# Routed experts on one Trainium2 core: the order of the 64-column and 32-column products over four weight blocks, and the places of the three small experts

## The chip, the cores and the metric

The kernel runs on one core of one Trainium2 chip, as a single program. The metric is the device time of one execution in microseconds (us), and less is better. The core's engines are TensorE (PE, with its weight loads shown as PEld), VectorE (DVE), ScalarE (ACT), GpSimd (POOL) and SyncE (SP), which issues nearly all transfers from HBM.

## The reference

A two-layer encoder trunk over 256 tokens of width 1024 in float32. Layer 0 is attention (two kinds of heads) and a dense SwiGLU; layer 1 is dilated window attention and a routed SwiGLU: each token goes to the two of eight experts with the highest router logits. Cut to the part that the change touches:

```python
def one_block(args):                       # the tokens of one expert
    tok, g, e = args
    xb = xt[tok]                           # (tokens, 1024)
    yb = (jax.nn.silu(xb @ wg[e]) * (xb @ wu[e])) @ wd[e]   # 1024 -> 3584 -> 1024
    return (yb.astype(jnp.float32) * g[:, None]).astype(h.dtype)
```

Each expert has 3 x 1024 x 3584 float32 weights, 44 MB, and 64 tokens on the mean. The output is x plus the gated sum of both experts of each token.

## The kernel before

The first third of the time goes to layer 0 and to the attention of layer 1. From 518 us on the kernel works through the eight experts one after another, in **places** e = 0 to 7. Place 0 always holds expert 7 (`FIRST`); the other seven experts are ranked on the chip by the number of their tokens, and `RANK` (line 28) says which rank stands in which place. The three smallest (ranks 0 to 2) stand in the places of `TWO` (line 26). What a place can hold is fixed when the program is built: 64 rows in a place of `TWO`, 96 in the others (`ROOM`, line 29). The shapes of all instructions so depend on the place and not on the data; tokens beyond the room go to `overflow`, behind an `If` at the end.

**Weights.** An expert's weights come as 42 loads of 1 MB each, all in the order of use and all issued on SP (line 221). Sixteen slots of 1 MB hold them (rings of 8, 2, 4 and 2); a load waits until the products that read its slot are done. Each load is two **blocks** of 128 x 1024 columns (`granules`, line 1040): 56 blocks for the gate and up projections (seven groups g of eight) and 28 for the down projection.

**Products.** The tokens are the stationary operand, the weights stream. For each block `products` (line 1278) goes through `parts(e)` (line 1229). The **wide part** takes tokens 0 to 63: two products with 64 stationary columns each, side by side in the array, each with half of the block's columns. A place with room for 96 also has the **narrow part**, tokens 64 to 95: four products with 32 stationary columns side by side, each with a quarter of the columns. float32 products run as two passes each, so in the trace a block is four wide matmuls of 512 columns, and then eight narrow ones of 256. Wide results gather in PSUM tiles psA (gate, up) and psD (down), narrow ones in psB.

**Between them on TensorE.** After each group g ScalarE and VectorE make h (lines 1310, 1311), and `turn` (line 1286) transposes it, with three 128-column products in a place with a narrow part and two in the others (line 1292). As written, `turn(g-1)` stands behind the fourth block of the next group, and `turn(6)` behind the third block of the down projection. `route` (line 1234) gathers the tokens of the next two places with 32 products (line 1251) and some small ones (line 1265); it is called by `ahead` in places 1, 3 and 5, as written behind block 18 of the down projection. At the end of a place `scatter` (line 1322) scales the result and adds it to the output by one indirect transfer for each part.

**Order.** Each engine runs its queue in order. The queue is laid out when the program is built, by a planner that goes through the instructions as they are written, but puts a later one ahead of an earlier one if, by the planner's own estimate of times, the earlier one still waits for its data. So the order in the trace can differ from the written one.

Of the kernel before, what the change touches and what calls it, by code (L numbers as in the profile page):

```python
# [20 lines left out]
KD = 8  # L21
# [1 line left out]
NE = 8  # L23
EPS = 1e-6
BIG = 4096.0
TWO = (1, 3, 5)
FIRST = NE - 1
RANK = (-1, 0, 3, 1, 4, 2, 5, 6)
ROOM = tuple(64 if j in TWO else 96 for j in range(NE))
RING = 8  # L30
NCONV = 3
# [148 lines left out]
def tile_trunk(ctx, tc, xT_d, fm_d, rw_d, ct_d, ada_et, ada_e, win_ab, win_c, uq_d, ukv_d, wout_e,  # L180
               ffn_gu, ffn_d, ada_ot, ada_o, qkv_d, wout_o, router_d, gu_d, wd_d, out, dbg=None):
    nc = tc.nc
    V, S, G, TE = nc.vector, nc.scalar, nc.gpsimd, nc.tensor
# [9 lines left out]
    def bank(tag):  # L193
        return psum.tile([P, 512], F32, tag=tag, name="ps" + tag, bufs={"A": 2, "D": 1, "B": 3, "C": 2}[tag])
# [40 lines left out]
    def F(n):  # L235
        return fm[:, FM[n][0]:FM[n][1]]
# [28 lines left out]
    for a in range(2):  # L265
        ps = bank("C")
        for b in range(4):
            k = 4 * a + b
# [102 lines left out]
    last = [None]  # L371
# [387 lines left out]
    for a in range(3):  # L759
        g = F("qn")[:, a:a + 1] if a < 2 else F("kvn")  # L760
# [14 lines left out]
    for k in range(2):  # L775
        w = stream.get()
# [14 lines left out]
    w = stream.get()  # L791
    for tt in range(2):
        for a in range(2):
            ps = bank("B")
# [6 lines left out]
    at = ExitStack()  # L801
# [88 lines left out]
    for f in range(22):  # L890
        ps = bank("A").rearrange("p (a b) -> p a b", a=2)
        for m in range(2):
            w = stream.get()
# [87 lines left out]
    at = ExitStack()  # L981
# [58 lines left out]
    def granules(j):  # L1040

        for make in [gu_load(j, g, kq) for g in range(7) for kq in range(4)] + [wd_load(j, pc) for pc in range(14)]:
            w = make()
            for lo in (0, 1024):
                yield w[:, lo:lo + 1024]

    stream.prime()
    first, stream = stream, Stream(cvm, wo[NCONV:])
# [16 lines left out]
    def wout():  # L1065
        for _ in range(NCONV):
            yield first.get()
        cvs.close()
        slots[0] = order()
        while True:  # L1070
            yield stream.get()

    wg = wout()
# [44 lines left out]
    rk8 = mb.tile([P, NE], F32, name="rk8")  # L1118
    for j, r in enumerate(RANK):
        G.memset(rt8[:, j:j + 1], float(r))  # L1120
# [3 lines left out]
    ps = bank("C")  # L1124
# [73 lines left out]
    def gates():  # L1198
# [14 lines left out]
        V.tensor_copy(eid, key)  # L1213
        V.tensor_scalar(cap, rk8, float(len(TWO)) - 0.5, -32.0, op0=ALU.is_lt, op1=ALU.mult)
        V.tensor_scalar(cap[:, :NR], cap[:, :NR], 96.0, None, op0=ALU.add)
# [13 lines left out]
    def parts(e):  # L1229


        return ((0, 64, 2),) if e in TWO else ((0, 64, 2), (64, 32, 4))

# [38 lines left out]
    def expert(e, xg, lo, mid, ahead):  # L1272


        wg = granules(e)
        hh, hts = {}, {}

        def products(outs, x, w, m, start, stop):
            for ps, (at, n, q) in zip(outs, parts(e)):
                c = 1024 // m // q  # L1280
                wv = w.rearrange("p (m c) -> p m c", m=m)
                for j in range(q):
                    TE.matmul(ps[n * j:n * j + n, :m * c].rearrange("p (m c) -> p m c", m=m), x(at, n),  # L1283
                              wv[:, :, j * c:(j + 1) * c], start=start, stop=stop, tile_position=(0, n * j))

        def turn(g):

            h = hh.pop(g)
            pt = bank("C")
            nb = 2 if e in TWO else 3  # L1290
            for b in range(nb):
                TE.transpose(pt[:, b * P:(b + 1) * P], h[:, b * P:(b + 1) * P], ident)  # L1292
            ht = mt.tile([P, 4, 96], F32, tag="ht%d" % g, name="ht")
            S.copy(ht[:, :, 0:64].rearrange("p (j b) t -> p b j t", b=2),  # L1294
                   pt[:, 0:256].rearrange("p (b j t) -> p b j t", b=2, j=2))
            if nb == 3:
                V.tensor_copy(ht[:, :, 64:96], pt[:, 256:384].rearrange("p (j t) -> p j t", j=4))  # L1297
            hts[g] = ht

        for g in range(7):  # L1300
            ps = [bank("A"), bank("B")][:len(parts(e))]
            for k in range(KD):
                products(ps, lambda at, n: xg[:, k, lo + at:lo + at + n], next(wg), 2, k == 0, k == KD - 1)
                if g and k == 3:
                    turn(g - 1)
                if g == 0 and k == 3 and mid:
                    mid()
            h = mt.tile([P, 384], F32, tag="hh", name="hh", bufs=2)
            for p, (at, w) in zip(ps, ((0, 256), (256, 128))):
                S.activation(h[:, at:at + w], p[:, 0:w], AF.Silu)  # L1310
                V.tensor_tensor(h[:, at:at + w], h[:, at:at + w], p[:, w:2 * w], op=ALU.mult)  # L1311
            hh[g] = h
        Y = [bank("D"), bank("B")][:len(parts(e))]
        for c in range(28):
            if c == 18 and ahead:
                ahead()
            products(Y, lambda at, n: hts[c // 4][:, c % 4, at:at + n], next(wg), 1, c == 0, c == 27)
            if c == 2:
                turn(6)
        return Y  # L1320

# [12 lines left out]
    for e in range(NE):  # L1334
        if e % 2 == 0:
            xg, at, back = nxt.pop()
        ahead = (lambda: nxt.append(route(e + 1))) if e % 2 and e + 1 < NE else None
        scatter(e, expert(e, xg, at[e % 2], None if e else g5_sum, ahead), back[e % 2])
# [104 lines left out]
```

## Time and profile before

| | us |
|---|---|
| runs, median of 3 | 1484.67 (1484.15 to 1487.27) |
| the profiled execution, its own time | 1487.64 |
| its span (first to last instruction) | 1485.8 |
| TensorE busy in the span | 1418.4 (95%) |
| experts, from the first product to the last | 518.4 to 1473.6 |
| weight transfers of the experts | 336 of 1 MB |

The profiled execution is 0.2% above the median. 1.84 us of its time lie outside the span. Matmuls are pipelined, so "busy" says only that some matmul was in flight; how long a block takes is read from where its first matmul and the next block's first matmul start.

### The profile page before, as it was taken

What the parts mean: (1) busy time and instruction counts of PE and PEld (TensorE: products, weight loads), DVE (VectorE), ACT (ScalarE), POOL (GpSimd) and SP (SyncE); (2) the same over time, 40 slices, a digit from 0 to 9 for tenths busy, and PEclk for the clock granted to TensorE, in tenths of its full rate; (3) what the DMA queues carried; (4) which work ended last, traced back from release to release, by engine and by line L of the source; (5) the groups of instructions that cost most, each with busy time, mean ns of one, the idle gap of its engine ahead of it and who ended that gap; (6) DMA issues with size and microseconds to landing.
All of it is one profiled execution on the core that took longest, in us unless ns stands there. A gap on an engine that the chain in (4) does not pass through costs nothing.

```text
span 1485.8 us, 23384 instructions
## 1 busy us (share of the span) xinstructions
PE 1418.4 (95%) x9779; PEld 647.5 (44%) x9779; DVE 433.6 (29%) x964; ACT 354.2 (24%) x750; POOL 51.1 (3%) x51
## 2 busy tenths in 40 slices
PE   6889999999989899999999998999998999999996
PEld 4646999998766722223322222322222322222221
DVE  5866787786886410000000000000000000000000
ACT  4557644445568310000100001100000100000000
POOL 0320000000020000000000000000000000000000
PEclk9989999999999899999999999999999999999998
DMA  9846678788432788999999999999999999999830
GB/s 393 341 155 251 212 285 299 284 306 308 161 114 91 295 336 321 320 331 415 421 418 420 378 331 419 421 417 421 351 333 410 421 414 421 367 326 335 317 140 11
DMA packets 67363, 472.11 MB, mean 318 GB/s; under 512 B 8145, under 2 KB 8593, under 8 KB 11185
## 3 DMA queue, kind: packets, MB, share of 16 engines
q1 hardware_dynamic: 64944, 467.34, 81.5%
q0 software_dynamic: 1872, 2.10, 0.9%
q8 instruction: 79, 1.29, 0.3%
q10 hardware_dynamic: 432, 1.08, 0.2%
q14 instruction: 36, 0.29, 0.1%
HBM read 467.34 MB, written 3.80 MB: 317 GB/s over the span
## 4 chain that ended last, share of the span: by engine, by line
issue 51%; PE 34%; DMA 7%; DVE 5%; ACT 2%; POOL 0%; POOLq 0%; SPq 0%; ACTq 0%; DVEq 0%
DMA out_dram<-acc,row 7%; PE psA L331 6%; PE psA L332 6%; PE psA L333 6%; PE psA L1283 4%; PE psB L1283 3%; PE psD L1283 2%; DVE wlo L355 1%; PE psD L610 1%; PE psB L315 1%; PE psC L596 1%; PE psB L562 1%; PE psA L562 1%; DMA w<-in_ada_ot_dram 1%; PE psC L1251 0%
## 5 line engine op out<-in xcount | busy, mean ns | idle before, releaser
L1283 PE MATMUL psA<-w,xg 128*64 128x512 f32 x1792 | 453.3, 612 | 0.0
L1283 PE MATMUL psD<-w,ht 128*64 128x512 f32 x896 | 229.3, 611 | 0.0
L1283 PEld LDWEIGHTS psA<-w,xg 128*64 128x64 f32 x1792 | 102.3, 136 | 196.9 <-issue 180.1
L1283 PE MATMUL psB<-w,xg 128*32 128x256 f32 x2240 | 180.8, 393 | 0.0
L1310 ACT ACTIVATE hh<-psA 128x256 f32<-128x256 f32 x56 | 21.5, 384 | 603.3 <-PE psA L1283 603.3
L355 DVE TENSOR_TENSOR wlo<-w,whi 128x1024 fp32r<-128x1024 f32 (+2 forms) x119 | 143.8, 1214 | 44.1 <-ACT whi L353 44.1
L1311 DVE TENSOR_TENSOR hh<-hh,psA 128x256 f32<-128x256 f32 x56 | 23.6, 421 | 452.2 <-ACT hh L1310 452.2
L1283 PEld LDWEIGHTS psB<-w,xg 128*32 128x32 f32 x2240 | 44.4, 108 | 227.7 <-issue 227.7
L353 ACT CAST whi<-w 128x1024 fp32r<-128x1024 f32 (+2 forms) x119 | 122.2, 1038 | 74.1 <-issue 30.0
L331 PE MATMUL psA<-h,whi 128*128 128x256 f32 x352 | 97.1, 277 | 0.2 <-ACT h L455 0.2
L332 PE MATMUL psA<-h,whi 128*128 128x256 f32 x352 | 97.1, 277 | 0.0
L333 PE MATMUL psA<-h,wlo 128*128 128x256 f32 x352 | 96.8, 276 | 0.0
L1283 PE MATMUL psB<-w,ht 128*32 128x256 f32 x1120 | 89.5, 391 | 0.0
L1283 PEld LDWEIGHTS psD<-w,ht 128*64 128x64 f32 x896 | 49.6, 135 | 90.2 <-issue 86.9
L1283 PEld LDWEIGHTS psB<-w,ht 128*32 128x32 f32 x1120 | 22.0, 108 | 113.6 <-issue 109.5
L1327 DVE SCALAR_TENSOR_TENSOR acc<-psD,gsl,g5a 128x512 f32<-128x512 f32 x8 | 6.0, 751 | 224.3 <-PE psD L1283 224.3
L331 PEld LDWEIGHTS psA<-h,whi 128*128 128x128 f32 x352 | 66.0, 188 | 0.6 <-ACT h L455 0.4
L332 PEld LDWEIGHTS psA<-h,whi 128*128 128x128 f32 x352 | 65.9, 188 | 0.3 <-DVE h L456 0.2
L333 PEld LDWEIGHTS psA<-h,wlo 128*128 128x128 f32 x352 | 65.9, 188 | 0.0
L1294 ACT COPY ht<-psC 128x256 f32<-128x256 f32 x56 | 20.9, 372 | 169.7 <-PE psC L1292 169.7
L1328 POOL DMA_INDIRECT out_dram<-acc,row x13 | 20.2, 1557 | 959.0 <-DVE acc L1327 923.4
L1297 DVE COPY ht<-psC 128x128 f32<-128x128 f32 x35 | 10.2, 292 | 141.6 <-ACT ht L1294 141.6
(335 smaller groups left out, 1583.5 us busy)
## 6 DMA issues: line engine op xcount, KB each, us to landing
w<-in_gu_dram SPq DMA_DIRECT2D x224, 1024.0 KB, 10.8
w<-in_wd_dram SPq DMA_DIRECT2D x112, 1024.0 KB, 11.1
w<-in_ada_e_dram SPq DMA_DIRECT2D x22, 1024.0 KB, 8.9
w<-in_ffn_gu_dram SPq DMA_DIRECT2D x22, 1024.0 KB, 5.1
w<-in_ada_ot_dram SPq DMA_DIRECT2D x16, 1024.0 KB, 4.9
w<-in_qkv_dram SPq DMA_DIRECT2D x12, 1024.0 KB, 6.6
w<-in_ffn_d_dram SPq DMA_DIRECT2D x11, 1024.0 KB, 6.6
w<-in_ada_o_dram SPq DMA_DIRECT2D x8, 1024.0 KB, 6.3
```

What stands on the lines that cost most here:

```text
L315: behind(TE.matmul(ps[32 * j:32 * j + 32], sc[:, 4 * i + j], w[:, j], start=i == 0, stop=i == 1, tile_position=(0, 32 * j)), after)
L331: TE.matmul(out_, a[0], b[0], start=start, stop=False)
L332: TE.matmul(out_, a[0], b[1], start=False, stop=False)
L333: TE.matmul(out_, a[1], b[0], start=False, stop=stop)
L353: behind(S.copy(hi[:, :n], w), self.after[0])
L355: self.last = V.tensor_tensor(lw, w, hi[:, :n].bitcast(F32), op=ALU.subtract)
L562: TE.matmul(bk[i][:, tt], q[:, tt * P:(tt + 1) * P], k, start=True, stop=True)
L1283: TE.matmul(ps[n * j:n * j + n, :m * c].rearrange("p (m c) -> p m c", m=m), x(at, n), wv[:, :, j * c:(j + 1) * c], start=start, stop=stop, ...
L1294: S.copy(ht[:, :, 0:64].rearrange("p (j b) t -> p b j t", b=2), pt[:, 0:256].rearrange("p (b j t) -> p b j t", b=2, j=2))
L1310: S.activation(h[:, at:at + w], p[:, 0:w], AF.Silu)
L1311: V.tensor_tensor(h[:, at:at + w], h[:, at:at + w], p[:, w:2 * w], op=ALU.mult)
L1328: G.indirect_dma_start(out=out.rearrange("t (j c) -> (t j) c", j=q), out_offset=bass.IndirectOffsetOnAxis(ap=row[:, 0:1], axis=0), in_=ys, ...
```

## The change

Within a group of four blocks all wide products come first, block after block, and then all narrow ones; in the places of `TWO`, which have no narrow part, the products keep their order. `turn(g-1)` is written behind the first four blocks as before, `turn(6)` behind the fourth block of the down projection instead of the third, and `ahead` behind block 16 instead of 18. The places without narrow part become 1, 4 and 7 (they were 1, 3 and 5), and `RANK` is set to fit, so that they still hold the three smallest of the seven ranked experts.

```diff
-TWO = (1, 3, 5)
+TWO = (1, 4, 7)
 FIRST = NE - 1
-RANK = (-1, 0, 3, 1, 4, 2, 5, 6)
+RANK = (-1, 0, 3, 4, 1, 5, 6, 2)
...
-        def products(outs, x, w, m, start, stop):
+        def products(outs, x, ws, m, first, last):
+
             for ps, (at, n, q) in zip(outs, parts(e)):
                 c = 1024 // m // q
-                wv = w.rearrange("p (m c) -> p m c", m=m)
-                for j in range(q):
-                    TE.matmul(ps[n * j:n * j + n, :m * c].rearrange("p (m c) -> p m c", m=m), x(at, n),
-                              wv[:, :, j * c:(j + 1) * c], start=start, stop=stop, tile_position=(0, n * j))
+                for i, w in ws:
+                    wv = w.rearrange("p (m c) -> p m c", m=m)
+                    for j in range(q):
+                        TE.matmul(ps[n * j:n * j + n, :m * c].rearrange("p (m c) -> p m c", m=m), x(i, at, n),
+                                  wv[:, :, j * c:(j + 1) * c], start=i == first, stop=i == last,
+                                  tile_position=(0, n * j))
...
-            for k in range(KD):
-                products(ps, lambda at, n: xg[:, k, lo + at:lo + at + n], next(wg), 2, k == 0, k == KD - 1)
-                if g and k == 3:
+            for k in range(0, KD, 4):
+                products(ps, lambda i, at, n: xg[:, i, lo + at:lo + at + n], [(i, next(wg)) for i in range(k, k + 4)],
+                         2, 0, KD - 1)
+                if g and k == 0:
                     turn(g - 1)
-                if g == 0 and k == 3 and mid:
+                if g == 0 and k == 0 and mid:
                     mid()
...
-        for c in range(28):
-            if c == 18 and ahead:
+        for g in range(7):
+            if g == 4 and ahead:
                 ahead()
-            products(Y, lambda at, n: hts[c // 4][:, c % 4, at:at + n], next(wg), 1, c == 0, c == 27)
-            if c == 2:
+            products(Y, lambda i, at, n: hts[i // 4][:, i % 4, at:at + n],
+                     [(i, next(wg)) for i in range(4 * g, 4 * g + 4)], 1, 0, 27)
+            if g == 0:
                 turn(6)
```

## Rows read from the trace of the kernel before

**Rows 1.** Sums by window, one window for each of places 0 to 3.
```profile
core 0: us, PE busy (x) PEld busy (x) DVE busy (x) ACT busy (x) POOL busy (x), PEclk, DMA share, GB/s
518.40:661.30 142.90, 142.90 (x1063) 33.99 (x1061) 10.04 (x31) 12.07 (x33) 0.00 (x0) 0.97 0.91 329
661.30:749.00 87.70, 83.32 (x420) 29.50 (x418) 4.66 (x16) 9.11 (x25) 3.27 (x2) 1.00 1.01 409
749.00:884.90 135.90, 135.90 (x1033) 31.96 (x1029) 8.23 (x23) 7.24 (x21) 1.54 (x1) 1.00 0.99 389
884.90:975.30 90.40, 83.19 (x418) 29.49 (x416) 4.70 (x16) 9.10 (x25) 3.09 (x2) 1.00 1.01 413
```
**Rows 2.** Waits of SP's queue in place 2: us in total, times, longest.
```profile
SPq L221 <- PE psB L1283: 69.4, 29, 3.1
```
**Rows 3.** Timeline of PE, one block of place 4: start us, us, engine, line.
```profile
999.42 1.08 PE L1283 MATMUL psA<-w,xg 128*64 128x512 f32 x4
1000.43 0.64 PE L1283 MATMUL psB<-w,xg 128*32 128x256 f32 x8
1001.00 1.08 PE L1283 MATMUL psA<-w,xg 128*64 128x512 f32 x4
```
**Rows 4.** Timeline of PE, the start of place 1, without narrow part.
```profile
661.27 10.52 PE L1283 MATMUL psA<-w,xg 128*64 128x512 f32 x48
671.72 0.44 PE L1292 MATMUL psC<-fm,hh 128*128 128x128 f32 x2
```
**Rows 5.** Timeline of PE, a run with 32 stationary columns in layer 0.
```profile
351.75 1.92 PE L315 MATMUL psB<-w,sc 128*32 128x512 f32 x16
353.60 0.60 PE L406 MATMUL psC<-ones,ssum 128*128 128x1 f32 x4
```
**Rows 6.** Timeline of PEld, the weight loads of the narrow part of Rows 3.
```profile
1000.42 0.16 PEld L1283 LDWEIGHTS psB<-w,xg 128*32 128x32 f32 x8 [0.81 <-issue]
```
**Rows 7.** Timeline of PE, the start of the down projection in place 0.
```profile
616.60 1.08 PE L1283 MATMUL psD<-w,ht 128*64 128x512 f32 x4
...
619.75 1.08 PE L1283 MATMUL psD<-w,ht 128*64 128x512 f32 x4
...
621.33 0.55 PE L1292 MATMUL psC<-fm,hh 128*128 128x128 f32 x3
```
**Rows 8.** Timeline of PE, the start of the down projection in place 2.
```profile
840.20 1.08 PE L1283 MATMUL psD<-w,ht 128*64 128x512 f32 x4
...
841.77 1.08 PE L1283 MATMUL psD<-w,ht 128*64 128x512 f32 x4
...
843.35 0.55 PE L1292 MATMUL psC<-fm,hh 128*128 128x128 f32 x3
```
**Rows 9.** Timeline of PE, the first group of place 3, without narrow part.
```profile
884.87 7.09 PE L1283 MATMUL psA<-w,xg 128*64 128x512 f32 x32
892.90 0.44 PE L1292 MATMUL psC<-fm,hh 128*128 128x128 f32 x2 [0.94 <-DVE hh L1311]
893.27 7.09 PE L1283 MATMUL psA<-w,xg 128*64 128x512 f32 x32
```
**Rows 10.** Timeline of PE, the down projection of place 3, with route.
```profile
943.72 1.94 PE L1283 MATMUL psD<-w,ht 128*64 128x512 f32 x8
945.59 0.79 PE L1251 MATMUL psC<-oh,htok 128*128 128x160 f32 x5
946.31 1.94 PE L1283 MATMUL psD<-w,ht 128*64 128x512 f32 x8
```
**Rows 11.** Timeline of all engines, the end of the span.
```profile
1472.95 0.64 PE L1283 MATMUL psB<-w,ht 128*32 128x256 f32 x8
1473.07 0.75 DVE L1327 SCALAR_TENSOR_TENSOR acc<-psD,gsl,g5a 128x512 f32<-128x512 f32 x1 [39.73 <-PE psD L1283]
...
1474.09 1.54 POOL L1328 DMA_INDIRECT out_dram<-acc,row  x1 [126.98 <-DVE acc L1327]
1480.69 1.54 POOL L1328 DMA_INDIRECT out_dram<-acc,row  x1 [5.06 <-DMA out_dram<-acc,row]
```

## Prediction

> **What bounds the kernel now.** I first took the sums by window, place by place. In place 2 TensorE has some matmul in flight for 135.90 of 135.90 us, and in place 3, which has no narrow part, for 83.19 of 90.40 us [rows 1]; the other engines are below 13 us in each. The only other candidate is the weight stream. Where TensorE is quick it runs at 409 to 414 GB/s; a load of 1.049 MB at 413 GB/s takes 2.54 us. In place 0 it runs at 329 GB/s, because it is held back: in place 2 SP waited 69.4 us for narrow products to give slots back [rows 1, 2]. So places with a narrow part are paced by TensorE. A place without one uses 42 loads in 90.40 us, in which 90.40 / 2.54 = 36 arrive: it lives on slots filled before, and the next place refills them. I read the whole stage as bound by what stands on TensorE's queue.
>
> Then the timeline of TensorE, for the price of a block. The wide part of a block takes 1000.43 - 999.42 = 1.01 us, the narrow part 1001.00 - 1000.43 = 0.57 us, together 1.58 us [rows 3]. In place 1 wide products stand alone: a run of 48 matmuls has a duration of 10.52 us, one of 32 has 7.09 us [rows 4, 9]. The difference, 3.43 us for four blocks, makes 0.86 us per wide part in a run. So a wide part between narrow ones pays 1.01 - 0.86 = 0.15 us for the change. The run of 48 pays as much before the 128-column transposes: 671.72 - 661.27 - 12 x 0.8575 = 0.16 us [rows 4].
>
> **The change, part by part.**
>
> *Price of a change on the narrow side.* The trace has no narrow run over several blocks. Its nearest row is a product of layer 0 with 32 stationary columns in four places, each pass 512 columns long: 16 matmuls, four passes one after another, take 353.60 - 351.75 = 1.85 us [rows 5]. With the change at the end (0.14 to 0.16 us) that is 0.43 us per pass of 512, thus 0.21 us per pass of 256 and 0.43 us per narrow part (two passes). The narrow part now takes 0.57 us, so 0.14 us is its own change. From below: a narrow run saves nothing, and a pair of changes (wide to narrow and back) is worth 0.15 us. From above: 0.15 + 0.14 = 0.29 us. I take 0.29 us, since the row with 32 columns shows the streamed pace, and keep both.
>
> *How many pairs go away.* Written out, four blocks have one pair instead of four. But the planner does not keep the written order where it expects a load to be late, and it did expect that from place 1 on. Three signs: `turn(6)`, written behind the third block of the down projection, stands behind three blocks in place 0 (616.60 to 621.33 us, 4.73 us = 3 x 1.58) and behind two in place 2 (840.20 to 843.35 us, 2 x 1.58) [rows 7, 8]. In place 3 a transpose written behind the twelfth block stands behind the eighth, though its h was not ready and TensorE stood still for 0.94 us [rows 9]. And `route`, written behind block 18, is cut into pieces of five between blocks, always after two blocks, which is one load [rows 10]. So the planner fills its gap at the border of a load with whatever is ready. In the new order the narrow products of a load's two blocks are ready at that very border, while the wide ones of the next load are not. I expect pairs over two blocks in places 2, 3, 5 and 6, and over four only in place 0, where the written order held.
>
> - Place 0: 84 blocks are 21 groups, three pairs less in each: 63 x 0.29 = 18.3 us.
> - Four places: 42 loads with one pair less in each: 168 x 0.29 = 48.7 us.
>
> A load's 2 x 1.58 = 3.16 us becomes 2.87 us, and such a place 135.9 - 12.2 = 123.7 us.
>
> *Places moved.* Three places without narrow part stay three, and the shapes hang on the place, so no work moves except `route`: two of its three calls now fall into places with a narrow part (3 and 5). There it stops between narrow and wide products, where a change is paid anyway; about eight stops at 0.15 us could give back some 2 us, and as many extra stops could take it. I take 0. Do the loads keep up? A place without narrow part and without `route` takes 90.4 us less the seven stops between two blocks' products that `route` makes in place 3, each 946.31 - 945.59 = 0.72 us plus about 0.15 [rows 10], and its small products: about 83 us. It uses 42 loads while 83 / 2.54 = 33 arrive, so it eats nine of sixteen slots; each place with a narrow part takes in 123.7 / 2.54 = 49 for 42, and two of them stand ahead of places 4 and 7. TensorE never waits for long: 0. If that cover were gone, such a place would take the time of its loads, 42 x 2.54 = 107 us instead of 83.
>
> *The end.* Now two parts are scattered, and the second transfer is issued 1480.69 - 1474.09 = 6.6 us after the first, behind its landing [rows 11]. With a place without narrow part last there is one. But VectorE's scaling of the wide result started at 1473.07, under narrow products that ran to 1473.59; without that cover the issue follows the last matmul by some 1.1 us instead of 0.5. From issue to the end it is 5.1 us (second transfer) to 6.6 (first): the last matmul is followed by 6.2 to 7.7 us instead of 1485.8 - 1473.6 = 12.2. I take 5 us off.
>
> *At nothing:* slots return after a load's last narrow part as now, and in place 0 two at a time, under a full ring; the transposes move by at most a block and take the same time wherever they stand; ScalarE gets psA earlier.
>
> Sum: 18.3 + 48.7 + 5 = 72 us. The profiled execution took 1487.64 us (span 1485.8 and 1.84 outside) and comes to 1415.6 us. The median of the runs is 2.97 us lower: 1484.67 - 72 = 1412.7, so 1413 us.
>
> **Rivals.**
>
> *Groups of four everywhere.* The planner finds two loads ready and keeps the written order. Another pair for each of 21 groups in four places: 84 x 0.29 = 24.4 us, thus 1388 us. For it: place 0 kept the written order. Against: all 28 transposes of places 2, 4, 6 and 7 stand at the border of a load ahead of where they are written, like the one of [rows 8].
>
> *The narrow run saves nothing.* 0.15 us for each of 231 pairs: 34.7 + 5 = 39.7 us, thus 1445 us. For it: passes of 256 columns in a row, 16 instructions with their loads in 0.43 us, stand nowhere in the trace. Against: the run of passes of 512 [rows 5].
>
> *Each narrow block's weight loads wait for the passes in front.* The eight loads of a narrow part take 0.16 us, with both passes' loads begun under the first pass [rows 6]; over several blocks it isn't shown. If each pass from the second block on stood still for its load of 0.11 us, a narrow part in a run would cost 0.43 + 0.22 = 0.65 us. A load's two blocks would take (2 x 0.86 + 0.15) + (0.57 + 0.65) = 3.08 instead of 3.16 us, four blocks 6.10 instead of 6.32: 168 x 0.08 + 21 x 0.22 + 5 = 23 us, thus 1462 us. The run of 48 wide matmuls and the run with 32 columns speak against it: both show four to 24 passes at 0.43 us with no such pause [rows 4, 5]. [...]
>
> *A transpose comes too early.* If in the four places the planner put each `turn` directly behind its group, as in place 3, 28 stops of 0.94 us [rows 9] would cost 26 us: 1439 us.
>
> *Loads become the bound.* If place 7 started with empty slots, it would take 107 instead of 83 us: 1437 us.
>
> [...]
>
> **How the numbers follow.** Forecast 0.56; four everywhere 0.20; narrow run saves nothing 0.08; waiting weight loads 0.04; early transposes 0.04; loads bound 0.03; slower by the clock 0.03; the gain lost otherwise 0.02. The range goes from four everywhere (1388, with 2 us for `route`'s stops) to the lower bound of the pair (1445): 1386 to 1445, with all cases but 0.09 inside. The forecast's own range is 1404 to 1424. A change under 0.2% (3 us) can't be told from none. Faster: 0.95; same 0.02; slower 0.03.
>
> **What would show it.** Right: in place 2 the timeline of TensorE has x8 wide and then x16 narrow, 2.87 us from one start to the next; in place 0 x16 and x32, 5.44 us; places with a narrow part near 124 us (with `route` near 131), those without near 83 (place 1 near 88); one indirect transfer at the end; granted clock at 1.00. Wrong: x16 and x32 in place 2 (then 1388), narrow runs slower than 0.43 us per block, idle time of TensorE ended by a transfer of weights in places 4 or 7. The prediction hangs most on how the planner orders the queue, which the trace of before shows only for other instructions than the ones now moved.

## The result, and the profile after

| | before | after |
|---|---|---|
| median, us | 1485.93 (1484.15 to 1487.27, 4 runs) | 1419.62 (1417.29 to 1420.14, 4 runs) |
| ratio | | 0.9551, 95% interval 0.9535 to 0.9568 |
| profiled execution / its span, us | 1487.64 / 1485.8 | 1419.45 / 1417.6 |

The median is 66 us lower; the forecast was 72 us (1413 us, range 1386 to 1445), from the 1484.67 us of the first three runs before. The profiled executions differ by 68.2 us in span.

Sums by window after the change, one window for each of places 0 to 7; the first four answer to [rows 1]:

```profile
521.80:645.00 123.20, 123.20 (x1061) 46.02 (x1061) 10.35 (x31) 12.02 (x33) 0.11 (x1) 0.98 0.96 374
645.00:733.00 88.00, 84.24 (x436) 29.39 (x434) 4.78 (x16) 9.48 (x26) 3.16 (x2) 1.00 1.02 415
733.00:858.30 125.30, 125.30 (x1033) 40.35 (x1029) 8.51 (x23) 7.24 (x21) 1.54 (x1) 1.00 1.01 419
858.30:989.00 130.70, 130.64 (x1099) 45.95 (x1095) 9.42 (x30) 11.05 (x32) 3.85 (x3) 1.00 0.92 339
989.00:1071.80 82.80, 76.22 (x354) 24.92 (x352) 3.43 (x8) 5.30 (x14) 2.33 (x2) 1.00 1.01 415
1071.80:1202.50 130.70, 130.64 (x1095) 46.05 (x1091) 8.99 (x26) 11.05 (x32) 2.25 (x2) 1.00 1.01 415
1202.50:1327.10 124.60, 124.60 (x1035) 41.26 (x1031) 8.24 (x23) 7.24 (x21) 2.38 (x2) 1.00 0.96 363
1327.10:1410.10 83.00, 76.41 (x354) 24.79 (x350) 3.44 (x8) 5.30 (x14) 3.09 (x2) 1.00 0.88 355
```

The forecast was 124.6 us for place 0, 123.7 for places 2 and 6, near 131 with `route` (3 and 5), near 83 for 4 and 7, near 88 for 1; every place is within 1.6 us of it. In places with a narrow part TensorE still has work in flight all the time, but for 0.06 us in each of places 3 and 5. The granted clock is 1.00 from place 1 on and 0.98 in place 0, where it was 0.97. The last column shows that the weights come faster in place 2 (419 GB/s, where it was 389). The stage takes 1410.1 - 521.8 = 888.3 us instead of 955.2.

The timeline of TensorE in place 2 shows what a load's two blocks look like now, to be held against the single block of [rows 3]:

```profile
763.30 1.94 PE L1285 MATMUL psA<-w,xg 128*64 128x512 f32 x8
765.17 1.07 PE L1285 MATMUL psB<-w,xg 128*32 128x256 f32 x16
766.17 1.94 PE L1285 MATMUL psA<-w,xg 128*64 128x512 f32 x8
768.04 1.07 PE L1285 MATMUL psB<-w,xg 128*32 128x256 f32 x16
769.05 0.44 PE L1295 MATMUL psC<-fm,hh 128*128 128x128 f32 x2
769.42 1.94 PE L1285 MATMUL psA<-w,xg 128*64 128x512 f32 x8
771.28 1.07 PE L1285 MATMUL psB<-w,xg 128*32 128x256 f32 x16
772.28 0.33 PE L1295 MATMUL psC<-fm,hh 128*128 128x128 f32 x1
772.54 1.94 PE L1285 MATMUL psA<-w,xg 128*64 128x512 f32 x8
```

Eight wide and sixteen narrow matmuls, two blocks and not four, and 2.87 us from one start to the next (763.30 to 766.17) instead of 3.16. The two narrow parts take 1.00 us, which is 2 x 0.43 + 0.14. One thing was not there before: the three transposes, together in [rows 8], are split, two after one load and one after the next, so that TensorE changes the width once more.

In place 0, where the written order held in [rows 7], it holds again, 5.45 us for four blocks (532.67 to 538.12):

```profile
532.67 3.65 PE L1285 MATMUL psA<-w,xg 128*64 128x512 f32 x16
536.26 1.93 PE L1285 MATMUL psB<-w,xg 128*32 128x256 f32 x32
538.12 3.65 PE L1285 MATMUL psA<-w,xg 128*64 128x512 f32 x16
```

Timeline of place 4, to be held against [rows 9], and of `route` in place 3, against [rows 10]:

```profile
988.95 7.09 PE L1285 MATMUL psA<-w,xg 128*64 128x512 f32 x32
996.98 0.44 PE L1295 MATMUL psC<-fm,hh 128*128 128x128 f32 x2 [0.94 <-DVE hh L1315]
```
```profile
946.05 1.94 PE L1285 MATMUL psD<-w,ht 128*64 128x512 f32 x8
947.92 1.07 PE L1285 MATMUL psB<-w,ht 128*32 128x256 f32 x16
948.92 0.34 PE L1251 MATMUL psC<-oh,htok 128*128 128x160 f32 x1
949.19 1.94 PE L1285 MATMUL psD<-w,ht 128*64 128x512 f32 x8
```

The transposes of a place without narrow part still come ahead of their data, and `route` now sits between a narrow and a wide run. The end, for [rows 11]: one transfer, issued at 1411.16, and the span ends 7.5 us after the last product (1410.1) instead of 12.2.

```profile
1410.14 0.75 DVE L1332 SCALAR_TENSOR_TENSOR acc<-psD,gsl,g5a 128x512 f32<-128x512 f32 x1 [24.73 <-PE psD L1285]
1411.16 1.54 POOL L1333 DMA_INDIRECT out_dram<-acc,row  x1 [71.48 <-DVE acc L1332]
```

### The profile page after: what moved, and what is told of

It is laid out like the page before. It is cut to its first block, busy times and chain, and to the rows that moved or that the text cites. A ratio compares the mean times of both kernels' runs of the same rounds, so it can differ in the third digit from the quotient of the medians.

```text
span 1417.6 us, 23384 instructions
## 1 busy us (share of the span) xinstructions
PE 1356.6 (96%) x9779; PEld 701.5 (49%) x9779; DVE 434.7 (31%) x964; ACT 354.6 (25%) x750; POOL 51.1 (4%) x51
## 4 chain that ended last, share of the span: by engine, by line
PE 86%; DVE 6%; issue 3%; DMA 2%; ACT 2%; POOL 0%; POOLq 0%; SPq 0%; ACTq 0%; DVEq 0%
PE psA L1285 27%; PE psB L1285 15%; PE psD L1285 14%; PE psA L331 6%; PE psA L332 6%; PE psA L333 6%; PE psC L1295 2%; PE psC L1251 1%; DVE wlo L355 1%; PE psD L610 1%; PE psB L315 1%; DMA w<-in_wd_dram 1%; DMA w<-in_gu_dram 1%; PE psC L596 1%; PE psB L562 1%
## 5 line engine op out<-in xcount | busy, mean ns | idle before, releaser
L1285 PE MATMUL psA<-w,xg 128*64 128x512 f32 x1792 | 420.3, 602 | 0.0
L1285 PEld LDWEIGHTS psA<-w,xg 128*64 128x64 f32 x1792 | 116.7, 137 | 214.0 <-issue 206.0
L1285 PE MATMUL psD<-w,ht 128*64 128x512 f32 x896 | 211.1, 600 | 0.0
L1285 PE MATMUL psB<-w,xg 128*32 128x256 f32 x2240 | 147.2, 384 | 0.0
L1285 PEld LDWEIGHTS psB<-w,xg 128*32 128x32 f32 x2240 | 60.6, 109 | 127.2 <-issue 99.8
L1285 PEld LDWEIGHTS psD<-w,ht 128*64 128x64 f32 x896 | 58.7, 136 | 104.6 <-issue 102.1
L331 PE MATMUL psA<-h,whi 128*128 128x256 f32 x352 | 98.7, 282 | 0.2 <-ACT h L455 0.2
L332 PE MATMUL psA<-h,whi 128*128 128x256 f32 x352 | 98.7, 282 | 0.0
L1285 PE MATMUL psB<-w,ht 128*32 128x256 f32 x1120 | 72.2, 384 | 0.0
L1285 PEld LDWEIGHTS psB<-w,ht 128*32 128x32 f32 x1120 | 30.5, 109 | 60.5 <-issue 46.2
```

The source lines that it names most:

```text
L331: TE.matmul(out_, a[0], b[0], start=start, stop=False)
L332: TE.matmul(out_, a[0], b[1], start=False, stop=False)
```

## The experiments

The theory: the gain is changes of the stationary width on TensorE, 0.15 us each, and the planner lets only half of the written grouping through outside place 0. The rivals: the moved places carry part of it; it isn't the width but any switch between two parts that costs; more grouping gives nothing or starves TensorE of weights. Medians are of runs on the same chip as the kernel before.

**The two halves of the change.** `e1_products_alone` is the changed kernel with the old places:

```diff
-TWO = (1, 4, 7)
+TWO = (1, 3, 5)
-RANK = (-1, 0, 3, 4, 1, 5, 6, 2)
+RANK = (-1, 0, 3, 1, 4, 2, 5, 6)
```

> The new order of the products with the old places (1, 3, 5 without narrow part). Theory (the pairs of changes are the gain, and the queue keeps them over two blocks): the experts' products take about 891 us instead of 955, and the end stays as before with its second transfer, so 4.7 us above the changed kernel: 1424 to 1426 us. Rival (the places keep the loads ahead): with one place between two without narrow part instead of two, TensorE waits for weights in places 3 or 5, and the time is 1435 us or more.

Measured: 1425.52 us (1422.3 to 1429.22), ratio 0.9574 (0.9541 to 0.9607). `e2_places_alone` is the kernel before with the new `TWO` and `RANK` (the diff turned round).

> The new places with the old order of the products. Theory: nothing but the shorter end, and two calls of route that fall into places with a narrow part: 1478 to 1482 us against 1486. Rival (the places carry a good part of the gain): 1460 us or less.

Measured: 1479.59 us (1478.29 to 1481.18), ratio 0.9942 (0.992 to 0.9964). The kernel before took 1488.67 us on this chip, so the products alone give 63 us and the places alone 9. Their sum, 72 us, is more than the 66 of both together, but the intervals (some 5 and 3 us either way) leave room for that. Of the 9 us, 4.6 are the shorter end in the profiles (7.6 us behind the last product instead of 12.2), and 2.5 are `route`: it lengthens the down projection by 6.2 to 6.4 us in a place with a narrow part, and by 7.5 in one without. In `e1_products_alone` no product of places 3 and 5 waits for weights, so at the pace of this kernel the new places are not needed to keep the loads ahead.

**More grouping than the planner lets through.** `e3_groups_of_four` ties every narrow product behind the last wide one of its four blocks (`behind` adds a dependency that fixes the order in the queue, without a semaphore; the diff is shortened):

```diff
+            wide = None
             for ps, (at, n, q) in zip(outs, parts(e)):
...
-                        TE.matmul(ps[n * j:n * j + n, :m * c].rearrange("p (m c) -> p m c", m=m), x(i, at, n),
+                        mm = TE.matmul(ps[n * j:n * j + n, :m * c].rearrange("p (m c) -> p m c", m=m), x(i, at, n),
...
+                        behind(mm, wide)
+                wide = mm
```

> As the changed kernel, but every narrow product is tied behind the last wide one of its four blocks, so that the queue can't be laid out load by load. Theory (0.29 us per pair of changes): 84 pairs less in places 2, 3, 5 and 6, 24 us: 1395 us; such a place takes about 119 us instead of 125. Rival (what is saved is the order within a load, and more of it gives nothing): 1419 us. Rival (waiting for two loads at once stops TensorE): above 1419 us, with idle time ended by transfers of weights.

Measured: 1393.94 us (1393.01 to 1396.0), ratio 0.9372 (0.9348 to 0.9396). The forecast was 1395 us. In place 2 the timeline now has whole groups:

```profile
765.80 1.94 PE L1286 MATMUL psA<-w,xg 128*64 128x512 f32 x8
767.67 1.93 PE L1286 MATMUL psB<-w,xg 128*32 128x256 f32 x32
769.53 3.65 PE L1286 MATMUL psA<-w,xg 128*64 128x512 f32 x16
773.11 1.93 PE L1286 MATMUL psB<-w,xg 128*32 128x256 f32 x32
774.98 1.94 PE L1286 MATMUL psA<-w,xg 128*64 128x512 f32 x8
```

The first and the last x8 are halves of a wide run that the three transposes cut in two. It is 5.45 us from wide run to wide run (769.53 to 774.98), as in place 0. So the price per pair holds a second time, and what the changed kernel left lying was left by the order of the queue.

**What the price is paid for.** `e5_same_width` is the kernel before, but the second part of a block takes tokens 0 to 63 again, with 64 stationary columns; tokens 64 to 95 are left out.

```diff
             for ps, (at, n, q) in zip(outs, parts(e)):
+                if at:
+                    at, n, q = 0, 64, 2
                 c = 1024 // m // q
```

> The kernel before, block by block, but the second part of each block takes tokens 0 to 63 again with 64 stationary columns in two positions instead of tokens 64 to 95 with 32 in four (so tokens 64 to 95 of each place are left out). Each block alternates between two sets of stationary columns and two PSUM tiles as before, but the width stays 64. Theory (the price is that of a change of width): a block takes 2 x 0.86 = 1.72 us, a place with a second part 148 us, the kernel 1543 to 1550 us. Rival (any change of the stationary columns' source or of the PSUM tile costs 0.15 us): a block takes 2.02 us, a place 173 us, the kernel 1665 to 1675 us.

Measured: 1539.06 us, one run, 4 us below the band. Places 2, 4, 6 and 7 take 148.6 to 148.8 us, as worked out; what the forecast left out is that places 1, 3 and 5 became 3 to 5 us shorter. In place 2 the timeline alternates between psA and psB, block part by block part:

```profile
799.93 1.03 PE L1285 MATMUL psB<-w,xg 128*64 128x512 f32 x4
800.79 1.03 PE L1285 MATMUL psA<-w,xg 128*64 128x512 f32 x4
801.65 1.03 PE L1285 MATMUL psB<-w,xg 128*64 128x512 f32 x4
802.50 1.03 PE L1285 MATMUL psA<-w,xg 128*64 128x512 f32 x4
```

0.86 us per part, the pace of a run of one kind in [rows 4]: switching to another PSUM tile, with the stationary columns loaded anew, costs nothing. (Within a block they are the same 64 columns again; from a block to the next they are others, at the same pace.) In [rows 3] the same wide part takes 1.01 us, and what differs is the part beside it: its width, and with it the number of products side by side, and the length of its passes, 256 columns instead of 512. The length by itself costs nothing, as a stretch of layer 0 in the kernel before shows, where the width stays at 128:

```profile
54.34 0.35 PE L332 MATMUL psA<-wlo,h 128*128 128x416 f32 x1
54.54 0.35 PE L333 MATMUL psA<-whi,h 128*128 128x416 f32 x1
54.73 0.40 PE L331 MATMUL psD<-whi,h 128*128 128x512 f32 x1
54.97 0.40 PE L332 MATMUL psD<-wlo,h 128*128 128x512 f32 x1
```

The matmul of 512 columns starts 0.19 us after the one of 416 in front of it, which is no more than from one of 416 to the next (0.20). So the change of width is the price, 0.14 to 0.16 us each by [rows 3 to 5]; the number of products side by side changes with it, and no run separates the two, nor shows what TensorE does in that time.

**Groups of eight.** `e4_groups_of_eight` has the ties and eight blocks in a group, `turn(g-1)` written behind them (shortened):

```diff
-            for k in range(0, KD, 4):
-                products(ps, ..., [(i, next(wg)) for i in range(k, k + 4)], 2, 0, KD - 1)
+            products(ps, ..., [(i, next(wg)) for i in range(KD)], 2, 0, KD - 1)
...
-        for g in range(7):
+        for g in range(0, 28, 8):
```

> As the run with groups of four tied, but groups of eight blocks, with the transposes of the group before written behind them. The queue as built splits those transposes (two and one) inside a run of wide products. Theory (0.15 us per change of width): ten pairs less in each of five places, 14.5 us, and two changes more for each of 28 groups because of the transposes, 8 us back: 1386 to 1391 us. Rival (a change costs nothing more where the run is long): 1394 us. Rival (four loads wanted at once stop TensorE): above 1394 us.

Measured: 1386.19 us (1384.5 to 1389.42), ratio 0.9322 (0.9293 to 0.935), as the count of changes says. `e6_eight_turn_behind` also ties the transposes; `done` is the last product of the group just written (shortened):

```diff
-                TE.transpose(pt[:, b * P:(b + 1) * P], h[:, b * P:(b + 1) * P], ident)
+                behind(TE.transpose(pt[:, b * P:(b + 1) * P], h[:, b * P:(b + 1) * P], ident), after)
...
-                turn(g - 1)
+                turn(g - 1, done)
```

> As the run with groups of eight, but each set of transposes is tied behind the last product of the group it is written behind, so it stands at the border to the next wide run, and in places without narrow part no longer ahead of its data. Theory: 14.5 us of pairs and one change for each of 28 groups, 4 us, against groups of four, and 17 stops of 0.94 us less: 1356 to 1362 us, places 4 and 7 at 76 us. Rival (loads become the bound): places without narrow part keep about 83 us or more, with idle time ended by transfers of weights: 1370 to 1385 us.

Measured: 1371.15 us (1370.23 to 1374.25), ratio 0.9226 (0.9201 to 0.9252): 9 us above the theory's band and at the foot of the rival's. The stops ahead of the transposes are gone, but places 4 and 7 take 80.5 and 80.8 us, between the theory's 76 and the rival's 83. In place 4 the timeline has TensorE waiting for weights in the down projection, which takes 29.3 us (1011.76 to 1041.09) instead of 24.1:

```profile
1011.76 7.09 PE L1286 MATMUL psD<-w,ht 128*64 128x512 f32 x32
1018.78 0.44 PE L1299 MATMUL psC<-fm,hh 128*128 128x128 f32 x2
1019.15 9.07 PE L1286 MATMUL psD<-w,ht 128*64 128x512 f32 x40
1028.66 1.51 PE L1286 MATMUL psD<-w,ht 128*64 128x512 f32 x6 [0.44 <-DMA w<-in_wd_dram]
```

The window of place 4 in this run has 418 GB/s, close to the 419 that are the most of any place in the changed kernel: here the loads have become the bound.

**Do the places matter then?** `e7_eight_turn_old_places` is that kernel with `TWO = (1, 3, 5)` and the old `RANK`.

> As the run before, but with the places 1, 3 and 5 without narrow part. Theory (two places with a narrow part are needed to refill what a faster place without one eats): the end is 4.7 us longer, and TensorE waits for weights in places 3 and 5: 1370 to 1385 us. Rival (the places matter for the end only): 5 us above the run before.

Measured: 1388.86 us (1387.04 to 1393.86), ratio 0.9351 (0.9322 to 0.938), 18 us above the run before and 4 us above the theory's band; the rival is out. The waits of TensorE:

```profile
PE psA L1286 <- DMA w<-in_gu_dram: 18.5, 34, 1.4
```

In the run before this row is 3.1 us. The theory had such waits in places 3 and 5 only (6.2 us each in this row); 3 us more stand at the start of each of places 4 and 6, which it had not. With the products of the changed kernel the new places are worth some 3 us (ratio 0.9551 against 0.9574 in `e1_products_alone`, intervals that overlap), and 18 us where TensorE is quicker.

**Groups of four with the transposes tied**, `e8_four_turn_behind`, and the run with groups of eight again, `e6b_eight_again`, on one chip:

> Groups of four tied as in the earlier run, and each set of transposes tied behind the first four blocks of the next group, where it is written. Theory (price of changes and stops alone): 28 groups with one change less than with groups of four, 4 us, and 17 stops of 0.94 us less: 1372 to 1376 us, thus 14 us above the sum for groups of eight by the same count, but within 5 us of what groups of eight measured, since there the loads took the rest. Places 2 and 6 at about 118 us, places 4 and 7 at 76 to 78 us. Rival (loads are the bound in both): the waits for weights in places 4 and 7 are as long as with groups of eight, and the time is 1380 us or more.

> The run with groups of eight and tied transposes once more, on the same chip as the one with groups of four: 1368 to 1374 us.

Measured: 1375.81 us (1375.1 to 1381.55), ratio 0.9265 (0.9237 to 0.9293), and 1372.75 us (1368.7 to 1377.66), ratio 0.9226 (0.9203 to 0.9248). Both are in their bands, and the two intervals overlap. With groups of four places 4 and 7 take 77.2 and 77.6 us, and TensorE waits 1.7 us for transfers of weights in the whole stage. With groups of eight place 2 is 2.1 us shorter (116.0 us instead of 118.1), but places 4 and 7 take 82.9 and 81.4 us and the waits are 8.5 us: a good part of the changes saved is paid back in waits for weights. The lowest ratio, 0.9226 in both runs with groups of eight and tied transposes, is 3.4% below the changed kernel's (0.9226 / 0.9551 = 0.966); whether it is below that of groups of four with tied transposes isn't shown.

## Why the prediction was right

1. **What bounds the kernel.** Right: the queue of TensorE. The gain came from the order of its products, and none of them waited for weights. There was not much room left, though: `e6_eight_turn_behind` ran into the loads at 418 GB/s, and place 2 of the changed kernel already takes 419.
2. **The price, 0.29 us per pair of changes, at the upper end of its bounds.** Right: 2.87 us per load and 5.45 us per four blocks, where 2.87 and 5.44 were worked out. The rival in which each narrow pass waits for its weight load is out, and so is the one in which the narrow run saves nothing: the narrow run of sixteen takes 1.00 us. The sixteen weight loads of that run (765.17 us in place 2) last 0.11 us each on the mean, and since 1.00 us is 2 x 0.43 + 0.14, it has no room for a stop at each of them. The granted clock stayed at 1.00 from place 1 on, and no transpose of places 2, 3, 5 and 6 waited for its data, so the case "slower by the clock", for which no run shows a sign, and the early transposes are out as well.
3. **Pairs over two blocks in places 2, 3, 5 and 6.** Right, but for three stretches that went in fours: the last 12 blocks of places 3 and 5, behind `route`, and the first 12 of place 6, nine groups in all. `e3_groups_of_four` shows that it was the queue's order and nothing of the chip. That the planner orders so because it expects a load to be late is inferred from the order alone, and why these nine groups kept theirs no run shows. Tied, places 2, 3, 5 and 6 are 488.7 us long together instead of 511.2, 22.5 us less, and the 84 - 9 = 75 pairs that were left to save are 75 x 0.29 = 21.8 us.
4. **Put at nothing, and wrong:** the transposes, which the prediction has "take the same time wherever they stand". They were split, which adds one change of width for 26 of 28 groups, 1.05 us in a place with seven. Places 2 and 6 are 1.6 and 0.9 us longer than worked out; place 6 has 0.9 us less to pay by its three groups in fours, so some 0.6 us in each stay unexplained. Place 0 is 1.4 us shorter than worked out, and that is luck with the clock. Its first microseconds ran at a granted clock of 0.50 before (the first line; the clock is the third figure from the end) and after (the second):

```profile
518.40:527.20 8.80, 8.80 (x56) 2.19 (x54) 1.17 (x7) 0.90 (x5) 0.00 (x0) 0.50 1.03 428
521.80:526.20 4.40, 4.40 (x35) 1.52 (x35) 0.32 (x2) 0.69 (x4) 0.00 (x0) 0.50 1.00 421
```

That is 8.8 us of place 0 before and 4.4 us after. The profiles of `e3_groups_of_four`, `e1_products_alone` and `e8_four_turn_behind`, with the very same order in place 0, have 5.4, 7.9 and 8.6 us at 0.50, and place 0 takes 123.7, 125.0 and 125.3 us: half a microsecond more for each microsecond at the lower clock. With 8.8 us it would have been some 125.4 us (an estimate from these rows), 0.8 us above the sum. So it is partly luck that the experts' 955.2 us fell by 66.9 us where the sum said 67.
5. **The places.** Right: no product of the experts waits for weights in the changed kernel, and `route` between narrow and wide products saves a change at its stops; it lengthens the down projection by 5.7 us in place 3 (46.1 against 40.4 in place 2) and by 7.8 us in place 1, without narrow part (31.9 against 24.1 in place 4). Of these 2.1 us, 0.9 are the three groups in fours of point 3; the other 1.2 us for each of the two calls that moved agree with the 2.5 us of `e2_places_alone`. The prediction named some 2 us for both and left them at 0.
6. **The end.** 4.7 us against 5.
7. **Not in the sum:** the experts started at 521.8 us instead of 518.4. The instructions ahead of them stand in the same order as before, and what differs is the pace of layer 0's products (see the last section). This makes the profiled 68.2 us out of 66.9 + 4.7 - 3.4.

## What to carry to other kernels

Read the cost of a switch as the difference between the same products in a run and among others, and then check in the order of the queue, not in the source, how many switches will be left: the signs were a transpose and a gather that stood ahead of where they were written, always at the border of a load. Group the products by the width of the stationary operand (0.29 us for each pair of changes saved here), and where a planner fills gaps with whatever it thinks is ready, tie the order down; after that look again at which engine or transfer ends last.

## What the runs showed that was not expected

Going back and forth between two PSUM tiles with stationary operands of one width costs nothing (0.86 us per part in `e5_same_width`), while a change of width cost 0.15 us from 64 to 32 columns, 0.14 us back (both by [rows 3 to 5]), 0.16 us from 64 to 128 ([rows 4]), and 0.15 us from 128 to 64 (in place 2 of the changed kernel two transposes take 0.37 us and one 0.26 us up to the next wide start, so 0.11 us each and 0.15 us once). And the same products of layer 0 have two paces at the same granted clock of 1.00: the 352 matmuls of line 331 that take h last 277 ns on the mean in eight of the eleven profiles, and 281 or 282 ns in three (the changed kernel, `e1_products_alone` and `e6b_eight_again`). In these three the experts start at 521.5 to 522.1 us, in the others at 516.3 to 520.0. Why there are two paces is not settled.
